# Value products with one 128-column stationary part, division in the merge, and logits in other PSUM banks

## The chip, the core and the metric

The kernel runs on one core of one Trainium2 chip. The metric is the device time in microseconds (us) from start to end of one execution; lower is better. The engines are TensorE (PE, matrix products), VectorE (DVE), ScalarE (ACT), GpSimd (POOL) and SyncE (SP, which issues transfers). ACT issues transfers too. All products here are made of float32 parts: a number x is split into a rounded high part and a low part x - high, and a product is the sum of high x high, high x low and low x high.

## The reference

One layer of a streaming encoder on 1088 frames (1024 of a prompt, 64 of a sample behind 128 cached ones), width 1024:

```python
h = x + 0.5 * swiglu(x, ffn1)
u = rms(h, mix_norm); z = u @ w_in              # q, k, v, indexer, conv input, gates
# attention: every query keeps its best keys by an indexer score (at most 256)
logits = einsum('bqcgd,bqncd->bqcgn', qg, kg) * HEAD_DIM ** -0.5
logits = where(valid, logits, -inf)
p = softmax(logits)
attn = einsum('bqcgn,bqncd->bqcgd', p, vg)      # 8 heads of 64, 2 key/value heads
conv_out = silu(layernorm(depthwise_conv(...))) @ conv_w_out
g_a, g_c = split(sigmoid(gate + b_gate), 2)
h = h + (g_a * (attn @ attn_w_out) + g_c * conv_out) @ w_out
h = h + 0.5 * swiglu(h, ffn2)
```

The change lies in the softmax, in the product with the values, and in how its result reaches `attn @ attn_w_out`.

## The kernel before

Frames are columns in most of the kernel, in three chunks (CHUNKS: 364, 362 and 362 wide, c = 0, 1, 2); the width of 1024 is 8 tiles of 128 partitions. The program goes: first feed-forward block, input projection, indexer scores and the search for the best keys on DVE, attention, second feed-forward block.

Attention runs over nine tiles of queries (eight of 128 in the prompt, number 8 of 64 in the sample; order TORD = 8, 5, 6, 7, 4, 3, 2, 1, 0, tile i with 128(i+1) keys) and, in each, over four pairs of heads. `soft` makes the logits of a pair: L999 and L1000 are the products of the queries with the high and low part of the keys, in a bank of the pool `lg`; L1002 adds the mask (0 or a large negative number) and takes the maximum over the keys on DVE; L1008 joins two halves of the maximum, L1010 scales it, L1012 is the exponential on ACT with its sum, L1014 the reciprocal of the sum on DVE, and L1016 multiplies the exponentials by it, for the first head of the pair on POOL and for the second on DVE. `turn` transposes the probabilities, two blocks of 128 keys at a time (L1026), and splits them into `ph` (ACT, L170) and `pl` (DVE, L171). `values` sums the product with the values in one bank, `pv`, by `mm3` (L154 to L156: high x ph, high x pl, low x ph, each with 64 stationary columns); L1052 copies the sum to `oh` on ACT, and L1053 sends it, from ACT's queue, to `d_at` in memory, head by head.

`attention` interleaves the pairs (logits two pairs ahead, value products two slots behind the transposes) and calls `fill` at each slot, which takes a few steps of a background program: the rest of the gates (L952 tanh on ACT, L953 to `d_g`), the convolution branch (L1132 to L1134, to `d_mp`), then the merge of chunk 2, its output projection, and the merge of chunk 1. A merge waits until the tiles of its chunk are done. It loads the attention result from `d_at` (L1150, `ar`) and splits it into `ah` and `al`, on DVE for even and POOL for odd k (L170, L171). For each of eight tiles m it loads the gate `ga` (L1157) and the convolution part `mpt` (L1159) on SP's queue, multiplies by the weights (`ps` from `ah` and `al`), joins both on DVE (L1162, L1163) and splits into `xh` and `xl` on ACT and DVE. `wout` multiplies these by w_out (24 products for each of 8 tiles m) and adds to h (L1175).

Behind the attention, h comes back from `d_h` in three large loads on ACT's queue (L1252); `wout` of chunk 1, the merge of chunk 0, its `wout` and the second feed-forward follow. Weights stream through `wload` all along: load `raw` on SP (L135), high part `whi` on ACT (L136), low part `wlo` on POOL (L137).

PSUM has eight banks. In the attention, `lg` has three, `psf` (background products) two, `psa` (transposes) two and `pv` one; pools take banks in the order in which they are opened. Each engine runs its own instructions in the order that the compiler's scheduler gives them, and each transfer waits for a completion counter where it takes one over from an earlier transfer; eight such counters are shared by SP's and ACT's queues.

Of the kernel before, what the change touches and what calls it, by code (L numbers as in the profile page):

```python
# [10 lines left out]
F32 = mybir.dt.float32  # L11
F32R = mybir.dt.float32r
# [8 lines left out]
P = 128  # L21
# [14 lines left out]
SC = 'PV'  # L36
# [74 lines left out]
class Kern:  # L111
# [342 lines left out]
    def run(self):  # L454
        tc, nc, a = self.tc, self.nc, self.a
        PS = bass.MemoryType.PSUM
        with ExitStack() as top:
# [10 lines left out]
            d_at = dram.tile([512, T], F32, name="d_at")  # L468
# [466 lines left out]
            vt = ak.tile([P, 2, 10, P], F32R, name="vt")  # L935
# [3 lines left out]
            self.split(vt[:, 0, 0:9, :], vt[:, 1, 0:9, :], raw[:, 0:9, :])  # L939
            self.split(vt[:SMP, 0, 9, :], vt[:SMP, 1, 9, :], raw[:SMP, 9, :])  # L940
# [23 lines left out]
            lgp = self.pool(at_es, "lg", NLG, space=PS)  # L964
            psf = self.pool(at_es, "psf", 7 - NLG - NPT, space=PS)
            psa = self.pool(at_es, "psa", NPT, space=PS)
            pvp = self.pool(at_es, "pv", 1, space=PS)
# [11 lines left out]
            def soft(u):  # L979

                rows, L = u.rows, u.L
                if u.h0 == 0 and u.i not in qts:
                    qts[u.i] = load_q(ak, d_q, u.t0, rows, (ak, ap_)[AORD.index(u.i) % 2], 1)
                qt = qts[u.i]
                nb = 2 if L > 512 else 1
                pw = L // nb
                mb = ap_.tile([P, 8, 2], F32, name="mb", tag="mb", bufs=AHEAD + 1)[:, 0:2, :]
                mx = ap_.tile([P, 2], F32, name="mx", tag="mx", bufs=AHEAD + 1)
                sm = ap_.tile([P, 2], F32, name="sm", tag="sm", bufs=AHEAD + 1)
                u.pr = []  # L990
                kh, kl = K[u.g]
                for hh in range(2):
                    p = ap_.tile([P, 1024], F32, name="pr", tag="pr", bufs=2 * AHEAD + 2)[:rows, :L]
                    u.pr.append(p)
                    q = qt[:, u.h0 + hh, :rows]
                    for b in range(nb):
                        o = lgp.tile([P, 512], F32, name="lg", tag="lg")[:rows, :pw]
                        ks = u.k0 + b * pw
                        nc.tensor.matmul(o, q, kh[:, ks:ks + pw], start=True, stop=False)  # L999
                        nc.tensor.matmul(o, q, kl[:, ks:ks + pw], start=False, stop=True)  # L1000
                        bo = BOFF[u.i] + b * pw
                        nc.vector.tensor_tensor_reduce(p[:, b * pw:(b + 1) * pw], o, bias[:rows, bo:bo + pw],  # L1002
                                                       1.0, -3e38, op0=ALU.add, op1=ALU.max,
                                                       accum_out=mb[:rows, hh, b:b + 1])
                        if (hh, b) == (1, nb - 1):
                            mm = mb[:rows, :, 0]
                            if nb == 2:
                                nc.vector.tensor_tensor(mx[:rows, :], mm, mb[:rows, :, 1], op=ALU.max)  # L1008
                                mm = mx[:rows, :]
                            nc.vector.tensor_scalar(mx[:rows, :], mm, -0.125, None, op0=ALU.mult)  # L1010
                            for e in range(2):
                                nc.scalar.activation(u.pr[e], u.pr[e], AF.Exp, bias=mx[:rows, e:e + 1],  # L1012
                                                     scale=0.125, accum_out=sm[:rows, e:e + 1])
                            nc.vector.reciprocal(sm[:rows, :], sm[:rows, :])  # L1014
                            for e in range(2):
                                {'P': nc.gpsimd, 'V': nc.vector}[SC[e]].tensor_scalar(u.pr[e], u.pr[e], sm[:rows, e:e + 1], None, op0=ALU.mult)  # L1016
                        yield
# [19 lines left out]

            def values(u, slot, ph, pl):
                first, last = slot[0] is u.blocks[0], slot[-1] is u.blocks[-1]
                n = 2 * u.rows  # L1040
                if first:
                    u.pv = pvp.tile([P, 512], F32, name="pv", tag="pv")[:64, 0:n]
                for s_, (vb, kk, kn) in enumerate(slot):
                    vh = vt[:kn, 0, vb, 64 * u.g:64 * u.g + 64]
                    vl = vt[:kn, 1, vb, 64 * u.g:64 * u.g + 64]
                    c = slice(n * s_, n * s_ + n)
                    self.mm3(u.pv, vh, vl, ph[:kn, c], pl[:kn, c], first and s_ == 0, last and s_ == len(slot) - 1)
                if last:
                    if u.h0 == 6:
                        done.add(u.i)  # L1050
                    oh = ap_.tile([64, 256], F32, name="oh", tag="oh", bufs=2)[:, :n]
                    nc.scalar.activation(oh, u.pv, AF.Copy)  # L1052
                    nc.scalar.dma_start(  # L1053
                        d_at[64 * u.h0:64 * u.h0 + 128, u.t0:u.t0 + u.rows].rearrange("(h d) c -> d h c", d=64),
                        oh.rearrange("d (h c) -> d h c", h=2))
# [87 lines left out]
            def merge(c, mp_):  # L1143
# [3 lines left out]
                al = mp_.tile([P, 4, WMAX], F32R, name="al", tag="al")[:, :, :w]  # L1147
                for k in range(4):
                    ar = mp_.tile([P, WMAX], F32, name="ar", tag="ar", bufs=2)[:, :w]
                    nc.sync.dma_start(ar, d_at[k * P:(k + 1) * P, c0:c0 + w])  # L1150
                    self.split(ah[:, k, :], al[:, k, :], ar, nc.gpsimd if k % 2 else nc.vector)
# [284 lines left out]
```

## Time and profile before

| | us |
|---|---|
| median of 3 runs | 2391.95 (2390.51 to 2393.91) |
| the profiled execution | 2394.14 |
| its span, first to last instruction | 2392.3 |
| search ends, first logits start (in the span) | 1151.6, 1157.5 |
| last value product starts | 1535.9 |
| wout of chunk 1 starts, merge of chunk 0 starts | 1540.0, 1574.9 |

The mean granted TensorE clock is 0.987 of full speed, and the chip moved 271.9 MB. The profile is of one execution; where it speaks of busy time, idle time of an engine counts only if another one waits for it.

### The profile page before, as it was taken

The page shows a single profiled execution, that of the slowest core. Times are in us where ns is not written, and L with a number is a line of the kernel's source. Part 1 is how long each engine was busy: PE and PEld are TensorE (multiplying, and loading weights), DVE is VectorE, ACT ScalarE, POOL GpSimd, SP SyncE. Part 2 cuts the span into 40 slices and gives each one's busy share as a digit, 9 for nine tenths or more (in the row PEclk, how much of TensorE's full clock was granted, in tenths as well). Part 3 has the DMA queues.
Part 4 walks back from the last instruction along what each step waited for, and adds up shares of the span by engine and source line. Part 5 has one row for each costly group of instructions (what it writes and reads, how often), then busy time and mean ns, then how long its engine had stood idle before and what let it go on. Part 6 is the DMA issues. An engine that isn't in the chain of part 4 may idle for free.

```text
span 2392.3 us, 43870 instructions
## 1 busy us (share of the span) xinstructions
PE 2300.3 (96%) x16762; PEld 2272.8 (95%) x16762; DVE 1658.8 (69%) x3606; ACT 1146.8 (48%) x2189; POOL 1407.1 (59%) x861
## 2 busy tenths in 40 slices
PE   5999999999999999999899899899999999999997
PEld 5999999999999999999898889899999999999997
DVE  7666678677567387579535897468766678776676
ACT  5433445444335546875644565345433445334343
POOL 4555556555556686889853455457455565445554
PEclk9999999999999999999999999999999999999999
DMA  4232332332223443333322446753232332332223
GB/s 166 89 104 91 98 98 90 125 107 98 89 90 121 143 138 121 91 120 120 106 78 96 125 135 204 254 167 113 80 100 92 107 103 72 108 108 97 89 98 117
DMA packets 130116, 271.90 MB, mean 114 GB/s; under 512 B 18032, under 2 KB 77296, under 8 KB 129904
## 3 DMA queue, kind: packets, MB, share of 16 engines
q1 hardware_dynamic: 114688, 253.48, 32.6%
q10 hardware_dynamic: 15216, 15.60, 2.0%
q8 instruction: 132, 2.16, 0.4%
q14 instruction: 80, 0.66, 0.1%
HBM read 230.34 MB, written 38.75 MB: 112 GB/s over the span
## 4 chain that ended last, share of the span: by engine, by line
PE 76%; DVE 9%; DMA 6%; POOL 4%; issue 2%; ACT 2%; SPq 0%; ACTq 0%; DVEq 0%; POOLq 0%
PE ps L154 24%; PE ps L156 24%; PE ps L155 24%; POOL ac L695 3%; DMA ga<-d_g 1%; PE pt L1026 1%; PE lgi L806 1%; PE lgi L807 1%; DMA d_h<-hr 1%; DVE ga L1163 1%; DMA raw<-wf 1%; DMA raw<-d_k 1%; PE ps L184 1%; DMA d_mp<-gc 1%; DVE t L229 1%
## 5 line engine op out<-in xcount | busy, mean ns | idle before, releaser
L137 POOL TENSOR_TENSOR wlo<-raw,whi 128x1024 fp32r<-128x1024 f32 (+1 forms) x187 | 435.9, 2335 | 352.3 <-ACT whi L136 343.5
L154 PE MATMUL ps<-x,wp 128*128 128x272 f32 x1760 | 508.4, 290 | 10.9 <-DVE spare L302 9.3
L155 PE MATMUL ps<-x,wp 128*128 128x272 f32 x1760 | 506.8, 289 | 0.0
L156 PE MATMUL ps<-x,wp 128*128 128x272 f32 x1760 | 506.1, 291 | 0.8 <-DVE wp L171 0.4
L154 PE MATMUL ps<-x,whi 128*128 128x272 f32 (+2 forms) x1544 | 483.1, 313 | 9.3 <-ACT x L170 4.3
L156 PE MATMUL ps<-x,wlo 128*128 128x272 f32 (+2 forms) x1544 | 481.2, 312 | 0.0
L155 PE MATMUL ps<-x,whi 128*128 128x272 f32 (+2 forms) x1334 | 412.7, 309 | 0.0
L154 PE MATMUL ps<-gh,whi 128*128 128x272 f32 x1408 | 399.8, 289 | 6.8 <-DVE spare L302 5.0
L155 PE MATMUL ps<-gl,whi 128*128 128x272 f32 x1408 | 404.7, 289 | 0.0
L156 PE MATMUL ps<-gh,wlo 128*128 128x272 f32 x1408 | 403.5, 288 | 0.0
L171 POOL TENSOR_TENSOR wlo<-raw,whi 128x1024 fp32r<-128x1024 f32 x88 | 220.4, 2505 | 261.6 <-ACT whi L170 253.2
L154 PEld LDWEIGHTS ps<-x,wp 128*128 128x128 f32 x1760 | 332.9, 189 | 11.7 <-ACT wp L170 11.6
L155 PEld LDWEIGHTS ps<-x,wp 128*128 128x128 f32 x1760 | 333.3, 189 | 0.0
L156 PEld LDWEIGHTS ps<-x,wp 128*128 128x128 f32 x1760 | 330.7, 189 | 2.5 <-DVE wp L171 2.1
L171 POOL TENSOR_TENSOR wp<-s,wp 128x512 fp32r<-128x512 f32 x176 | 256.6, 1458 | 97.2 <-ACT wp L170 97.2
L154 PEld LDWEIGHTS ps<-x,whi 128*128 128x128 f32 x1544 | 293.2, 190 | 11.3 <-ACT x L170 4.7
L136 ACT ACTIVATE whi<-raw 128x1024 fp32r<-128x1024 f32 (+1 forms) x187 | 190.6, 1020 | 218.1 <-PE ps L155 116.8
L156 PEld LDWEIGHTS ps<-x,wlo 128*128 128x128 f32 x1544 | 293.3, 190 | 0.9
L442 DVE SCALAR_TENSOR_TENSOR h<-ps,h 128x272 f32<-128x272 f32 x384 | 164.3, 438 | 184.9 <-PE ps L156 184.4
L695 POOL TENSOR_TENSOR ac<-ac,pd 128x559 f32<-128x559 f32 x180 | 260.9, 1449 | 35.2 <-ACT pd L694 11.8
L154 PEld LDWEIGHTS ps<-gh,whi 128*128 128x128 f32 x1408 | 262.9, 189 | 8.3 <-DVE spare L302 5.7
L156 PEld LDWEIGHTS ps<-gh,wlo 128*128 128x128 f32 x1408 | 265.7, 189 | 0.0
(238 smaller groups left out, 4782.0 us busy)
## 6 DMA issues: line engine op xcount, KB each, us to landing
raw<-wf SPq DMA_DIRECT2D x334, 512.0 KB, 3.3
raw<-wf SPq DMA_DIRECT2D x32, 384.0 KB, 3.1
d_g<-sg ACTq DMA_DIRECT2D x32, 181.0 KB, 1.9
d_h<-h SPq DMA_DIRECT2D x2, 2176.0 KB, 10.4
y<-t SPq DMA_DIRECT2D x32, 136.0 KB, 1.8
raw<-d_q SPq DMA_DIRECT2D x32, 128.0 KB, 2.7
raw<-d_qi SPq DMA_DIRECT2D x24, 128.0 KB, 3.0
d_g<-sg ACTq DMA_DIRECT2D x16, 182.0 KB, 1.9
```

Source lines behind the costliest of these rows:

```text
L136: nc.scalar.activation(hi[:, :n], raw[:, :n], AF.Copy)
L137: self.weng.tensor_tensor(lo[:, :n], raw[:, :n], hi[:, :n], op=ALU.subtract)
L154: t.matmul(out, wh, xh, start=first, stop=False)
L155: t.matmul(out, wh, xl, start=False, stop=False)
L156: t.matmul(out, wl, xh, start=False, stop=last)
L171: (eng or nc.vector).tensor_tensor(lo, x, hi, op=ALU.subtract)
L184: self.nc.tensor.matmul(ps[:, b * P:(b + 1) * P], x[:, t0:t0 + P], self.ones, start=i == 0, stop=i == len(tiles) - 1)
L229: self.nc.vector.scalar_tensor_tensor(x, h[:, k, t0:t0 + w], self.par[:, q:q + 1], r, op0=ALU.mult, op1=ALU.mult)
L442: nc.vector.scalar_tensor_tensor(x, p, 0.5, x, op0=ALU.mult, op1=ALU.add)
L695: nc.gpsimd.tensor_tensor(ac, ac, pd, op=ALU.add)
L806: nc.tensor.matmul(o, qt[:, hd, :], kih[:, ks:ks + pw], start=True, stop=False)
L807: nc.tensor.matmul(o, qt[:, hd, :], kil[:, ks:ks + pw], start=False, stop=True)
```

## The change

One product takes the place of two: the stationary side is now the high and the low part of the values side by side, 64 columns each, so that a product with `ph` gives high x ph in partitions 0 to 63 and low x ph in 64 to 127, and one with `pl` likewise (low x pl comes in too). The two halves go to `d_at` apart, twice the bytes, and are added in the merge.

The probabilities are no longer divided. The reciprocals of a tile's eight heads are collected in `rs`, transposed once a tile on PE, copied on ACT to `rt8` and sent to `d_rs` as rows; the merge loads them over 64 partitions each (`rw`) and multiplies. The merge now has two loads of 64 partitions for each `ar`, an addition and a multiplication for each k, on DVE for even and POOL for odd k. The maximum is found as the minimum of the logits times -0.125, which needs no joining and scaling. `oh` has four buffers for two. The pool `lg` is opened behind `psf` and `psa`, so the three pools swap banks.

```diff
-            d_at = dram.tile([512, T], F32, name="d_at")
+            d_at = dram.tile([8, P, T], F32, name="d_at")
+            d_rs = dram.tile([8, T], F32, name="d_rs")
...
-            vt = ak.tile([P, 2, 10, P], F32R, name="vt")
+            vt = ak.tile([P, 10, 2, 2, 64], F32R, name="vt")
...
-            lgp = self.pool(at_es, "lg", NLG, space=PS)
             psf = self.pool(at_es, "psf", 7 - NLG - NPT, space=PS)
             psa = self.pool(at_es, "psa", NPT, space=PS)
+            lgp = self.pool(at_es, "lg", NLG, space=PS)
...
-                        nc.vector.tensor_tensor_reduce(p[:, b * pw:(b + 1) * pw], o, bias[:rows, bo:bo + pw],
-                                                       1.0, -3e38, op0=ALU.add, op1=ALU.max,
-                                                       accum_out=mb[:rows, hh, b:b + 1])
-                        if (hh, b) == (1, nb - 1):
...
-                            nc.vector.reciprocal(sm[:rows, :], sm[:rows, :])
-                            for e in range(2):
-                                {'P': nc.gpsimd, 'V': nc.vector}[SC[e]].tensor_scalar(u.pr[e], u.pr[e], sm[:rows, e:e + 1], None, op0=ALU.mult)
+                        nc.vector.tensor_tensor_reduce(p[:, b * pw:(b + 1) * pw], o, bias[:rows, bo:bo + pw], -0.125,
+                                                       mn[:rows, hh, 0:1] if b else 3e38,
+                                                       op0=ALU.add, op1=ALU.min, accum_out=mn[:rows, hh, b:b + 1])
+                        if b == nb - 1:
+                            nc.scalar.activation(p, p, AF.Exp, bias=mn[:rows, hh, b:b + 1], scale=-1.0,
+                                                 accum_out=sm[:rows, hh:hh + 1])
+                            if hh:
+                                nc.vector.reciprocal(rs[:, u.h0:u.h0 + 2], sm[:rows, :])
...
-                    self.mm3(u.pv, vh, vl, ph[:kn, c], pl[:kn, c], first and s_ == 0, last and s_ == len(slot) - 1)
+                    vv = vt[:kn, vb, u.g, :, :].rearrange("p a d -> p (a d)")
+                    nc.tensor.matmul(u.pv, vv, ph[:kn, c], start=first and s_ == 0, stop=False)
+                    nc.tensor.matmul(u.pv, vv, pl[:kn, c], start=False, stop=last and s_ == len(slot) - 1)
                 if last:
                     if u.h0 == 6:
                         done.add(u.i)
+                        pt = psa.tile([P, 512], F32, name="pt", tag="pt")[:8, :u.rows]
+                        nc.tensor.transpose(pt, rss[u.i][:u.rows], ident[:u.rows, :u.rows])
+                        rt = ap_.tile([8, P], F32, name="rt8", tag="rt8", bufs=2)[:, :u.rows]
+                        nc.scalar.activation(rt, pt, AF.Copy)
+                        nc.scalar.dma_start(d_rs[:, u.t0:u.t0 + u.rows], rt)
-                    oh = ap_.tile([64, 256], F32, name="oh", tag="oh", bufs=2)[:, :n]
+                    oh = ap_.tile([P, 256], F32, name="oh", tag="oh", bufs=4)[:, :n]
...
+                rs = mp_.tile([P, 4, WMAX], F32, name="rw", tag="rw")[:, :, :w]
+                for e in range(2):
+                    nc.sync.dma_start(rs[64 * e:64 * e + 64],
+                                      d_rs.rearrange("(k e) c -> e k c", e=2)[e:e + 1, :, c0:c0 + w].to_broadcast([64, 4, w]))
                 for k in range(4):
-                    ar = mp_.tile([P, WMAX], F32, name="ar", tag="ar", bufs=2)[:, :w]
-                    nc.sync.dma_start(ar, d_at[k * P:(k + 1) * P, c0:c0 + w])
-                    self.split(ah[:, k, :], al[:, k, :], ar, nc.gpsimd if k % 2 else nc.vector)
+                    ar = mp_.tile([P, 2, WMAX], F32, name="ar", tag="ar", bufs=2)[:, :, :w]
+                    for e in range(2):
+                        nc.sync.dma_start(ar[64 * e:64 * e + 64],
+                                          d_at[2 * k + e, :, c0:c0 + w].rearrange("(a d) c -> d a c", a=2))
+                    eng = nc.gpsimd if k % 2 else nc.vector
+                    eng.tensor_tensor(ar[:, 0, :], ar[:, 0, :], ar[:, 1, :], op=ALU.add)
+                    eng.tensor_tensor(ar[:, 0, :], ar[:, 0, :], rs[:, k, :], op=ALU.mult)
+                    self.split(ah[:, k, :], al[:, k, :], ar[:, 0, :], eng)
```

The code that the diff does not touch keeps its text, but the scheduler gives some of it another place. At the end of the attention ACT's order before is this (`oh` is the copy of the last value products, `d_at<-oh` its transfer, `h<-d_h` the three loads of h, `xh` the split of the merge of chunk 1):

```order
1253 L1052 ACTIVATE oh<-pv 64x256
1254 L170 ACTIVATE ah<-ar 128x364
1255 L1053 DMA d_at<-oh 64x2x128
1256 L170 ACTIVATE xh<-ga 128x362
1257 L1052 ACTIVATE oh<-pv 64x256
1258 L1252 DMA h<-d_h 128x8x362
1259 L1053 DMA d_at<-oh 64x2x128
1260 L1252 DMA h<-d_h 128x8x362
1261 L170 ACTIVATE xh<-ga 128x362
1262 L1252 DMA h<-d_h 128x8x364
1263 L218 ACTIVATE acc<-h 128x272
```

And with the change, at the same place (lines have moved: L1055, L1056 and L1264 are what L1052, L1053 and L1252 were):

```order
1291 L169 ACTIVATE xh<-ga 128x362
1292 L135 ACTIVATE whi<-raw 128x1024
1293 L1055 ACTIVATE oh<-pv 128x256
1294 L1264 DMA h<-d_h 128x8x362 x2
1295 L1056 DMA d_at<-oh 128x2x128
1296 L1264 DMA h<-d_h 128x8x364
1297 L169 ACTIVATE xh<-ga 128x362
1298 L217 ACTIVATE acc<-h 128x272
1299 L169 ACTIVATE xh<-ga 128x362
```

Two loads of h now stand ahead of the last transfer to `d_at`, and two splits of the merge of chunk 1 behind all three. On PE, around the last value product, the order before goes straight on to wout of chunk 1 (operands `xh`, `xl`):

```order
9925 L154 MATMUL pv<-ph,vt 64x256
9926 L155 MATMUL pv<-pl,vt 64x256
9927 L156 MATMUL pv<-ph,vt 64x256
9928 L154 MATMUL ps<-xh,whi 128x362
9929 L155 MATMUL ps<-xl,whi 128x362
9930 L156 MATMUL ps<-xh,wlo 128x362
```

With the change, products of the merge of chunk 1 (operands `ah`, `al`) come first:

```order
9760 L1044 MATMUL pv<-ph,vt 128x256
9761 L1045 MATMUL pv<-pl,vt 128x256
9762 L153 MATMUL ps<-ah,whi 128x362
9763 L154 MATMUL ps<-al,whi 128x362
9764 L155 MATMUL ps<-ah,wlo 128x362
```

What moved is the last two tiles of that merge, 24 products in all, from ahead of the last value product to behind it; wout of chunk 1 follows them. Their loads on SP, in the order with the change (the loads of 362 columns are of chunk 1, m = 6 and 7; those of 364 of chunk 0, where `ar` stands for k = 1, 2 and 3):

```order
287 L1158 DMA ar<-d_at 64x2x364 x2
288 L134 DMA raw<-wf 128x1024
289 L1171 DMA mpt<-d_mp 128x362
290 L1169 DMA ga<-d_g 128x362
291 L1171 DMA mpt<-d_mp 128x362
292 L1169 DMA ga<-d_g 128x362
293 L1158 DMA ar<-d_at 64x2x364 x2
294 L134 DMA raw<-wf 128x1024
295 L1158 DMA ar<-d_at 64x2x364 x2
```

Before, the last loads of 362 columns stand ahead of the second half of the `ar` loads, and nothing of a load of h is waited for in front of them:

```order
281 L1150 DMA ar<-d_at 128x364
282 L1159 DMA mpt<-d_mp 128x362 x2
283 L1157 DMA ga<-d_g 128x362
284 L1150 DMA ar<-d_at 128x364
285 L135 DMA raw<-wf 128x1024
286 L1157 DMA ga<-d_g 128x362
287 L1159 DMA mpt<-d_mp 128x364
```

In the changed program as built, the mpt loads in rows 289 and 291 wait on the completion counters that the first and the second load of h raise, the raw load in row 294 on that of the third.

More of the change, by code (lines that the diff above doesn't have):

```diff
@@ L938, in run @@
             nc.sync.dma_start(raw[:SMP, 9, :], d_v[:SMP, 9, :])
-            self.split(vt[:, 0, 0:9, :], vt[:, 1, 0:9, :], raw[:, 0:9, :])
-            self.split(vt[:SMP, 0, 9, :], vt[:SMP, 1, 9, :], raw[:SMP, 9, :])
+            for g in range(2):
+                for r, b in ((P, slice(0, 9)), (SMP, slice(9, 10))):
+                    self.split(vt[:r, b, g, 0, :], vt[:r, b, g, 1, :], raw[:r, b, 64 * g:64 * g + 64])
             AORD = TORD
@@ L986, in soft @@
                 pw = L // nb
-                mb = ap_.tile([P, 8, 2], F32, name="mb", tag="mb", bufs=AHEAD + 1)[:, 0:2, :]
-                mx = ap_.tile([P, 2], F32, name="mx", tag="mx", bufs=AHEAD + 1)
+                mn = ap_.tile([P, 2, 2], F32, name="mn", tag="mn", bufs=AHEAD + 1)
                 sm = ap_.tile([P, 2], F32, name="sm", tag="sm", bufs=AHEAD + 1)
+                if u.h0 == 0:
+                    rss[u.i] = ap_.tile([P, 8], F32, name="rs", tag="rs", bufs=2)
+                rs = rss[u.i][:rows]
                 u.pr = []
@@ L1036, in turn @@
                 return ph, pl
+            rss = {}
             def values(u, slot, ph, pl):
@@ L1041, in values @@
                 if first:
-                    u.pv = pvp.tile([P, 512], F32, name="pv", tag="pv")[:64, 0:n]
+                    u.pv = pvp.tile([P, 512], F32, name="pv", tag="pv")[:, 0:n]
                 for s_, (vb, kk, kn) in enumerate(slot):
-                    vh = vt[:kn, 0, vb, 64 * u.g:64 * u.g + 64]
-                    vl = vt[:kn, 1, vb, 64 * u.g:64 * u.g + 64]
                     c = slice(n * s_, n * s_ + n)
-                    self.mm3(u.pv, vh, vl, ph[:kn, c], pl[:kn, c], first and s_ == 0, last and s_ == len(slot) - 1)
+                    vv = vt[:kn, vb, u.g, :, :].rearrange("p a d -> p (a d)")
+                    nc.tensor.matmul(u.pv, vv, ph[:kn, c], start=first and s_ == 0, stop=False)
+                    nc.tensor.matmul(u.pv, vv, pl[:kn, c], start=False, stop=last and s_ == len(slot) - 1)
                 if last:
@@ L1050, in values @@
                         done.add(u.i)
-                    oh = ap_.tile([64, 256], F32, name="oh", tag="oh", bufs=2)[:, :n]
+                        pt = psa.tile([P, 512], F32, name="pt", tag="pt")[:8, :u.rows]
[4 more added lines that the diff above has]
+                    oh = ap_.tile([P, 256], F32, name="oh", tag="oh", bufs=4)[:, :n]
                     nc.scalar.activation(oh, u.pv, AF.Copy)
                     nc.scalar.dma_start(
-                        d_at[64 * u.h0:64 * u.h0 + 128, u.t0:u.t0 + u.rows].rearrange("(h d) c -> d h c", d=64),
-                        oh.rearrange("d (h c) -> d h c", h=2))
+                        d_at[u.h0:u.h0 + 2, :, u.t0:u.t0 + u.rows].rearrange("h p c -> p h c"),
+                        oh.rearrange("p (h c) -> p h c", h=2))
             def attention(units, fill):
```

9 lines of the change are left out of this document (removed).

## The prediction, made before the changed kernel was run

> **What bounds the kernel now.** First the head of the page and its chain of waits; then busy time by stage, for the stretch that the change touches: the attention with its background work (1150 to 1540 us of the span) and the start of what follows.
>
> ```profile
> span 2392.3 us, 43870 instructions
> PE 2300.3 (96%) x16762; PEld 2272.8 (95%) x16762; DVE 1658.8 (69%) x3606; ACT 1146.8 (48%) x2189; POOL 1407.1 (59%) x861
> PE 76%; DVE 9%; DMA 6%; POOL 4%; issue 2%; ACT 2%; SPq 0%; ACTq 0%; DVEq 0%; POOLq 0%
> ```
>
> TensorE (PE) is busy for 96% of the span and holds 76% of the chain, so over the whole run an edit counts by the PE time that it frees. In the stretch at issue that isn't so everywhere (columns: stretch and its length; busy us of PE, its weight loads, DVE, ACT and POOL, that is VectorE, ScalarE and GpSimd; granted clock, DMA share, GB/s):
>
> ```profile
> 1160.00:1290.00 130.00, 130.00 (x835) 126.45 (x835) 51.05 (x140) 69.23 (x134) 72.93 (x43) 0.99 0.27 84
> 1290.00:1420.00 130.00, 115.81 (x824) 107.04 (x822) 117.60 (x302) 81.90 (x170) 63.13 (x31) 1.00 0.45 135
> 1420.00:1490.00 70.00, 66.36 (x425) 64.78 (x425) 55.93 (x132) 37.50 (x90) 38.52 (x24) 0.96 0.56 174
> 1490.00:1540.00 50.00, 41.96 (x248) 40.43 (x246) 25.74 (x39) 18.21 (x32) 27.39 (x14) 0.95 0.68 218
> ```
>
> Call the rows A, B, C and D. In A, PE is never idle. In B DVE is busy for 117.60 of 130 us and PE stands still for 14.2. In C and D PE stands still for 11.7 us, and most of what it waits for is this (between 1150 and 1620 us: total, times, longest):
>
> ```profile
> PE ps L154 <- DVE ga L1162: 7.8, 5, 3.8
> PE pv L154 <- ACT oh L1052: 6.7, 4, 3.5
> ```
>
> **The value products.** The order of the changed kernel has two products of 256 columns where there were three (304 for 456), each with 128 stationary columns for 64. How many stood in each stretch (PE, weight loads, ACT), and how far apart products start:
>
> ```profile
> 1160.00:1290.00 130.00, 15.27 (x113) 13.16 (x114) 2.54 (x8) 0.99 0.27 84
> 1290.00:1420.00 130.00, 41.02 (x250) 29.93 (x248) 5.14 (x14) 1.00 0.45 135
> 1420.00:1490.00 70.00, 12.05 (x72) 9.25 (x71) 2.92 (x8) 0.96 0.56 174
> 1490.00:1540.00 50.00, 3.93 (x24) 2.91 (x24) 2.19 (x6) 0.95 0.68 218
> ```
>
> ```profile
> 1244.76 0.28 PE L154 MATMUL pv<-ph,vt 128*64 128x256 f32 x1
> 1245.35 0.28 PE L156 MATMUL pv<-ph,vt 128*64 128x256 f32 x1
> 1699.87 0.29 PE L154 MATMUL ps<-x,whi 128*128 128x272 f32 x1
> 1701.38 0.29 PE L154 MATMUL ps<-x,whi 128*128 128x272 f32 x1
> ```
>
> Between the first two rows lie five steps (0.118 us each), between the others, with 128 stationary and 272 moving columns, twelve (0.126 us): 0.46 ns a moving column in both, so the wider load lies under the product before it. I take it at 0 to 3 ns each (under 1 us in all). A third of the products is freed: 113/3 x 0.118 = **4.4 us in A**, 9.8 in B, 3.8 in C and D.
>
> One rule speaks against this edit. The Trainium skill, "TensorE: Matmul & The Clock Gate", section "LDWEIGHTS (loading the stationary operand)", has the load grow with its columns, at P/1.2 ns: 53 ns for 64, 107 for 128 (an estimate by that page). Were it not hidden, 304 x 53 ns = 16 us would eat what 152 fewer products save (rival 4). The trace agrees on the growth but shows the longer load hidden, with its 0.126 us a step.
>
> **The normalisation.** The change takes away the 36 + 36 multiplications at L1016 and the maxima and scalings at L1008 and L1010. Their cost in B, L1016 (DVE, then POOL) and L1010 (DVE); then the spread of L1010 (ns: least, median, most) and that of operations like those that come:
>
> ```profile
> 1290.00:1420.00 130.00, 8.15 (x13) 32.99 (x14) 1.00 0.45 135
> 1290.00:1420.00 130.00, 5.05 (x14) 1.00 0.45 135
> L1010 DVE TENSOR_SCALAR mx<-mb x20: 151/306/2342, 1160.6 to 1515.1; 128x2 f32<-128x2 f32 x16, 64x2 f32<-64x2 f32 x4
> L171 DVE TENSOR_TENSOR al<-ar,ah x6: 525/538/1683, 1341.0 to 1549.3; 128x362 fp32r<-128x362 f32 x4, 128x364 fp32r<-128x364 f32 x2
> L171 POOL TENSOR_TENSOR al<-ar,ah x6: 970/1099/1258, 1354.7 to 1559.7; 128x362 fp32r<-128x362 f32 x4, 128x364 fp32r<-128x364 f32 x2
> ```
>
> In B DVE loses 8.15 + 5.05 = 13.2 us and the few of L1008. The merge's additions and multiplications come in its place: 12 on DVE and 12 on POOL, of the shape of the last two rows, some 4 of DVE's in B: 2.2 us, 3 with stretching as in the 1683 ns case. DVE is 10.2 us shorter, PE 9.8. Between 9.8 (PE alone gains) and 24 (its 14.2 idle us go as well) I take **14 us in B**, near the DVE figure plus some of the 32.99 us of POOL that go from the path from reciprocal to transpose. That an operation on two elements took 2342 ns, where 151 is the least, shows what DVE suffers from something beside it.
>
> The Trainium skill, "SBUF — State Buffer", section "Who interferes with whom", names POOL's exclusive lock on a port pair as the cause of such stretching. By it POOL's 33 us would give DVE time back beyond its own instructions. The 2342 ns agree; how much it is, no run here shows (rival 5).
>
> In C and D: 3.8 for the products plus some of the 11.7 idle us. But there SP's loads for the merge double in number (ar: two of 64 partitions for one of 128, and rw) and wait for landings ahead of the ga and mpt loads that PE waits for (first row of the waits). Between 0 and 13 I take **6.5**.
>
> **The start.** The 6.9 us at L999 end with the last tanh of the gates:
>
> ```profile
> 1157.50 0.42 PE L999 MATMUL lg<-kh,qt 128*64 128x192 f32 x1 [6.88 <-ACT sg L952]
> 1158.52 0.56 PE L154 MATMUL ps<-x,whi 128*128 128x364 f32 x1
> ```
>
> With the logits in other banks the six between these rows no longer wait for it. The gates' product of the second row does, since its pool takes the banks that the logits had; only 1.02 us move: **1 us** (0 to 1.5).
>
> **Small costs.** Nine transposes of reciprocals, with a wait each, and the wider loads: **1.7 us** (0.6 to 3). ACT's nine copies and DMA issues lie beside PE; where ACT is late they cost what the L1052 waits cost now, within those bounds.
>
> **The tail.** This is the term that decides. Rows of PE, ACT's queue, ACT and DVE behind the last value product, SP's wait for h loads, and a ga load's time to landing:
>
> ```profile
> 1535.93 0.28 PE L156 MATMUL pv<-ph,vt 128*64 128x256 f32 x1
> 1539.98 0.64 PE L154 MATMUL ps<-xh,whi 128*128 128x362 f32 x1 [3.77 <-DVE ga L1162]
> 1574.69 0.33 PE L156 MATMUL ps<-xh,wlo 128*128 128x362 f32 x1
> 1574.85 0.33 PE L154 MATMUL ps<-ah,whi 128*128 128x364 f32 x1
> ...
> 1537.96 0.57 ACTq L1252 DMA_DIRECT2D h<-d_h  x1
> 1540.44 5.10 ACTq L1252 DMA_DIRECT2D h<-d_h  x1
> 1548.08 0.43 ACT L218 ACTIVATE acc<-h 128x272 f32<-128x272 f32 x1 [7.14 <-DMA h<-d_h]
> 1554.98 0.98 DVE L1175 SCALAR_TENSOR_TENSOR h<-ps,h 128x362 f32<-128x362 f32 x2 [4.05 <-DMA h<-d_h]
> ```
>
> ```profile
> SPq L1159 <- DMA h<-d_h: 4.5, 1, 4.5
> ```
>
> ```profile
> ga<-d_g SPq DMA_DIRECT2D x2, 181.0 KB, 3.2
> ```
>
> Before, the wout products of chunk 1 start 4.05 us after the last value product and last 34.9, up to the first merge product of chunk 0. All loads that they need were issued ahead of the h loads, which land 10.1 us (the first) and 17.0 (the second) after the first was issued. In the order of the changed kernel two merge tiles of chunk 1 (m = 6 and 7: 24 products, 3.9 us by the step of 0.16 from 1574.69 to 1574.85) stand behind the last value product, and their loads behind h: as the kernel is built, SP's mpt load of m = 6 waits for the completion counter that h load 1 raises, that of m = 7 for h load 2's, with ga of m = 7 behind it. The row of SP's waits shows it in such a wait already. The first h load is issued 0.8 us behind the last value product, with one copy ahead of it (2.0 before), so h load 2 lands 14 to 18 us behind it (14 if less traffic beside it makes it quicker), the two loads 3.2 us later, two DVE steps and a split some 1.3 more: wout starts 18.5 to 22.5 us after the last value product, and its 34.9 us end at 53.4 to 57.4 where they ended at 38.9. That is **16.5 us lost** (11 if the loads have the queues to themselves, 20 if SP is late as well). The 3.9 us of merge products stood ahead of the last value product before and now lie inside this wait, so the stretch ahead is shorter by **3.9 us**. Nothing else fills the wait, since PE keeps its order.
>
> **Sum.** -4.4 - 14 - 6.5 - 1 - 3.9 + 1.7 + 16.5 = -11.6 us. Against the profiled execution (2394.14 us, of which 2392.3 is span) that is 2382.5; it lies 2.19 us above the median of 2391.95, so the time forecast is **2380 us**.
>
> **Rivals.**
> 1. The tail is hidden: the h loads land early, or the counters don't couple. For it: SP, held up, sends little beside them. Against it: 10.1 and 17.0 us above. All but the tail remains, -28.1: 2364 us. Chance 0.15.
> 2. Only PE's own saving counts, and DVE's and POOL's relief comes to nothing, since new loads on SP take over as what PE waits for. For it: five waits for ga, 7.8 us. Against it: DVE's 90% in B. -4.4 - 9.8 - 3.8 - 1 - 3.9 + 1.7 + 16.5 = -4.7: 2387 us. Chance 0.18.
> 3. Slower: the tail grows at one place. In the changed order SP's load of ar for k = 3 stands behind a weight load that waits for h load 3 (issued 1540.44 and landed 21.0 us later, below), and POOL does that part's add, multiply and split ahead of twelve weight splits. wout's fifth tile, due 16 us after wout starts (36.6 us behind the last value product), needs the first of these. h load 3 lands 0.8 + 2.5 + 21.0 = 24.3 us behind that product if it lands as before, ar 4.7 later and with its issue at about 30; POOL's own part of 3 to 4 us and one split of 2.4 make 36.4: just in time. Each us later costs one. From a landing at 46.5 on (11.6 to lose, and 4.8 more) it decides; at 50 it gives 2400 us. For it: d_at's traffic doubles (2.2 to 4.4 MB each way). Against: in the rows of before only h itself lands so late. Chance 0.13.
>
> ```profile
> h<-d_h ACTq DMA_DIRECT2D x1, 1456.0 KB, 21.0
> ar<-d_at SPq DMA_DIRECT2D x4, 182.0 KB, 4.7
> 1557.33 2.40 POOL L137 TENSOR_TENSOR wlo<-raw,whi 128x1024 fp32r<-128x1024 f32 x1 [2.33 <-ACT whi L136]
> ```
>
> 4. The weight loads aren't hidden. A load of 64 columns takes 134 ns, one of 128 takes 190, so 304 x 56 ns = 17 us come back: 2397 us. Against it: the steps of 0.126 us above. Chance 0.04.
>
> ```profile
> L154 PEld LDWEIGHTS pv<-ph,vt x152: 129/134/223, 1179.2 to 1535.6; 128*64 128x64 f32 x148, 64*64 64x64 f32 x4
> L154 PEld LDWEIGHTS ps<-x,whi 128*128 128x128 f32 x1544 | 293.2, 190 | 11.3 <-ACT x L170 4.7
> ```
>
> 5. POOL's work is what stretches DVE, so that all of PE's idle time in B goes with it: 24 us there for 14. For it: 2342 ns against 151. Against it: POOL gets 12 of the merge's additions and multiplications and keeps its 2.4 us weight splits. 2370 us. Chance 0.10.
>
> That the change doesn't do what it says is out: its order has 304 products on 128 columns.
>
> **From these to the numbers.** Forecast 0.40 (2373 to 2386 by itself). Of that nearly all is faster by over 0.2%, which is 4.8 us and about what a measurement of this kernel tells from no change; of rival 2 under half. Faster 0.38 + 0.15 + 0.07 + 0.10 = 0.70; same 0.02 + 0.11 + 0.02 (the edge of 3) = 0.15; slower 0.11 + 0.04 = 0.15. The range leaves out the quick half of rival 1 and the far part of 3 and 4: 2363 to 2395.
>
> **What would show it.** In the changed profile: value products x304 starting every 0.12 us (else rival 4); DVE in the second stretch well under 117 us and few PE waits there; the first wout product 18 to 23 us behind the last value product, with PE idle most of it and the wait ending with DVE's ga, and SP waiting for h<-d_h. If PE is idle there for under 5 us, rival 1 holds and the time is near 2364. If wout itself stops at its fifth tile for POOL's wlo, it's rival 3. If the stretch up to the last value product is shortened by under 22 us, the terms for B, C and D are wrong.

## The result, and the profile after

| | before | changed |
|---|---|---|
| median, 4 runs each (us) | 2391.23 (2384.43 to 2393.91) | 2412.54 (2408.60 to 2416.82) |
| ratio, 95% interval | | 1.0094 (1.0066 to 1.0121) |
| profiled execution, its span (us) | 2394.14, 2392.3 | 2408.60, 2406.8 |

The changed kernel is 0.94% slower, some 21 to 22 us (21.3 by the medians, 22.5 by the ratio); 2380 was forecast, with a range up to 2395. The profiled execution of the changed kernel is the fastest of its four, 3.9 us below their median.

The head of its page, the busy rows of the same stretches as before, and the longest waits of PE between 1150 and 1640 us:

```profile
PE 2297.5 (95%) x16619; PEld 2269.4 (94%) x16619; DVE 1625.7 (68%) x3532; ACT 1149.7 (48%) x2200; POOL 1355.7 (56%) x837
```

```profile
1160.00:1290.00 130.00, 130.00 (x822) 126.33 (x820) 40.43 (x113) 70.75 (x142) 52.13 (x32) 0.99 0.30 96
1290.00:1420.00 130.00, 114.01 (x746) 105.05 (x745) 113.77 (x277) 82.77 (x176) 34.06 (x22) 0.95 0.51 147
1420.00:1490.00 70.00, 59.53 (x368) 57.29 (x367) 43.39 (x104) 34.59 (x87) 26.39 (x14) 0.95 0.68 195
1490.00:1540.00 50.00, 42.71 (x233) 41.78 (x231) 14.90 (x24) 14.40 (x22) 25.64 (x12) 0.87 0.82 241
```

```profile
PE ps L153 <- DVE ga L1174: 19.9, 6, 8.6
PE ps L153 <- ACT sg L953: 5.5, 1, 5.5
PE pt L1022 <- DVE pl L170: 4.5, 6, 2.1
PE ps L153 <- DVE hr L1187: 3.2, 1, 3.2
```

The reader is to see three things. PE has 143 products less, and DVE and POOL are busy for less time, as intended (PE's busy time falls by 2.8 us only, since a product that runs slower counts as longer). In the second stretch DVE is still busy for 113.77 of 130 us, and PE's granted clock is 0.95 where it was 1.00. And the waits for ga went from 7.8 to 19.9 us.

To see where the time went, both traces were cut at equal work: the products other than value products and reciprocals' transposes are the same in both, so their moving columns were counted from 1115 us on, where the two run alike. The table (worked out from all PE rows of the two traces) gives for each stretch of the kernel before the time that the same work took in each. "own" is the value products and reciprocals at their usual step, "idle" PE's idle time, "slow" what products took above their usual step, at a lower clock or for another reason.

```
stretch of before   before: took  own  idle slow   changed: took  own  idle slow   difference
1160 to 1290        129.9  12.2   0.0   6.2        127.2   9.0   0.0   6.5          -2.7
1290 to 1420        130.3  28.7  14.2  12.1        128.9  19.1  16.0  18.3          -1.4
1420 to 1490         69.8   8.2   3.6   6.5         77.4   6.5  10.5   9.0          +7.6
1490 to 1520         29.7   1.4   0.6   0.9         31.9   0.7   2.8   1.7          +2.2
1520 to 1550         30.0   1.4   7.4   5.3         41.5   0.2  16.1   9.3         +11.5
```

At 1160 us the two were level (0.1 us), at 1550 the changed kernel is 17 us behind. In the second stretch 9.6 us of products are gone and 8.0 come back as idle and slow time. The third loses 7.6 us, the end 11.5. Over the five stretches 16.4 us of products are saved, PE is idle for 19.6 us more, and slow time is 13.8 us more.

Such a cut is of one execution, and neighbouring stretches trade time when the order changes: e4 below, which as a whole takes as long as the kernel before, is by the same cut 6.0 us shorter in the second stretch and 6.8 us longer in the third. So a stretch shows where time went in that execution; what an edit costs is read from the whole times.

The end, first on PE, then on ACT's queue, ACT and DVE, then SP's waits for h between 1525 and 1580 us:

```profile
1531.14 0.28 PE L1044 MATMUL pv<-ph,vt 128*128 128x256 f32 x1
1531.26 0.28 PE L1045 MATMUL pv<-pl,vt 128*128 128x256 f32 x1
1535.60 0.67 PE L153 MATMUL ps<-ah,whi 128*128 128x362 f32 x1 [4.05 <-DVE ga L1174]
1542.99 0.67 PE L153 MATMUL ps<-ah,whi 128*128 128x362 f32 x1 [3.40 <-DVE ga L1174]
1555.61 0.64 PE L153 MATMUL ps<-xh,whi 128*128 128x362 f32 x1 [8.63 <-DVE ga L1174]
1590.64 0.33 PE L153 MATMUL ps<-ah,whi 128*128 128x364 f32 x1
...
1531.64 0.59 ACTq L1264 DMA_DIRECT2D h<-d_h  x1
1533.78 6.28 ACTq L1056 DMA_DIRECT2D d_at<-oh  x1
1544.09 0.43 ACT L217 ACTIVATE acc<-h 128x272 f32<-128x272 f32 x1 [2.17 <-DMA h<-d_h]
1533.80 1.30 DVE L1162 TENSOR_TENSOR ar<-ar,rw 128x364 f32<-128x364 f32 x1 [6.15 <-DMA rw<-d_rs]
1541.96 0.54 DVE L170 TENSOR_TENSOR xl<-ga,xh 128x362 fp32r<-128x362 f32 x1 [5.84 <-ACT xh L169]
1554.93 0.53 DVE L1174 SCALAR_TENSOR_TENSOR ga<-ga,ps 128x362 f32<-128x362 f32 x1 [3.08 <-DMA ga<-d_g]
```

```profile
SPq L1171 <- DMA h<-d_h: 10.1, 2, 7.4
```

wout of chunk 1 starts 24.4 us behind the last value product (4.05 before; 18.5 to 22.5 forecast) and its end, the first merge product of chunk 0, lies 59.4 us behind it (38.9 before; 53.4 to 57.4 forecast). SP's mpt loads wait for the h loads, as the order showed, and the last and longest of PE's three waits (8.63 us) ends with them, when ga of m = 7 has landed. The first two have other sources that the forecast hadn't: DVE's multiplication for the next merge waits 6.15 us for rw ahead of the eviction for which PE waits until 1535.60; and the d_at transfer holds ACT's queue for 6.28 us, with the split xh behind it, for which DVE waits 5.84 us ahead of the eviction for which PE waits until 1542.99.

In the third stretch, rows of DVE and PE, and DVE's longest wait between 1420 and 1490 us:

```profile
1484.57 0.54 DVE L1161 TENSOR_TENSOR ar<-ar 128x362 f32<-128x362 f32 x1 [5.39 <-DMA ar<-d_at]
1485.60 0.53 DVE L1187 SCALAR_TENSOR_TENSOR hr<-ps,hr 128x362 f32<-128x362 f32 x1
1486.18 0.67 PE L153 MATMUL ps<-xh,whi 128*128 128x362 f32 x1 [3.24 <-DVE hr L1187]
```

```profile
DVE ar L1161 <- DMA ar<-d_at: 8.2, 2, 5.4
```

DVE's new addition waits for ar ahead of the eviction L1187, and PE for that eviction, 3.24 us. DVE has no wait for ar or rw between 1420 and 1490 us in the kernel before.

### The profile page after: what moved, and what is told of

Same layout as the page of the kernel before. It is cut to its first block, busy times and chain, and to the rows that moved or that the text cites. A ratio compares the mean times of both kernels' runs of the same rounds, so it can differ in the third digit from the quotient of the medians.

```text
span 2406.8 us, 43499 instructions
## 1 busy us (share of the span) xinstructions
PE 2297.5 (95%) x16619; PEld 2269.4 (94%) x16619; DVE 1625.7 (68%) x3532; ACT 1149.7 (48%) x2200; POOL 1355.7 (56%) x837
## 4 chain that ended last, share of the span: by engine, by line
PE 78%; DVE 9%; DMA 6%; POOL 3%; issue 2%; ACT 2%; SPq 0%; ACTq 0%; DVEq 0%; POOLq 0%
PE ps L153 25%; PE ps L155 24%; PE ps L154 24%; POOL ac L695 3%; DMA ga<-d_g 1%; PE pt L1022 1%; DVE pl L170 1%; PE lgi L806 1%; PE lgi L807 1%; DMA h<-d_h 1%; DVE ga L1175 1%; PE ps L183 1%; DVE pr L1005 1%; DMA raw<-d_k 1%; DVE t L228 1%
```

## The experiments

All were timed in five rounds against the kernel before; "x us" is the ratio times 2392. Comparisons of two experiments are good to some 4 us, the width of their intervals. Where an edit makes the order of h fixed, it is this one (m = 7 is the last tile of the merge of chunk 1):

```diff
+        self.hi = nc.scalar.activation(hi, x, AF.Copy)            # in split
...
+                    if (c, m) == (1, 7):
+                        self.mark = self.hi                       # in merge
...
+                self.behind(nc.scalar.dma_start(h[...], d_h[...]), self.mark)
```

### The tail, the products, the division and the banks apart

e1_h_last is the changed kernel with that edit.

> The changed kernel; only the three loads of h are issued behind the last ACT split of the merge of chunk 1 (m = 7). Theory A: the wait behind the last value product comes from the h loads in front of the last d_at transfer and from the ga and mpt loads of m = 6 and 7 that wait for them. Then wout of chunk 1 starts 6 to 10 us after the last value product (24.5 in the changed kernel), the first merge product of chunk 0 40 to 46 us after it (59.4), and the time falls by 12 to 18 us, to 2395 to 2400 us. Rival: merge loads are late because of their own number and traffic, wherever h stands: wout still starts 18 us or more after the last value product, and the time stays within 5 us of the changed kernel's 2412.

Measured: 1.0050 (1.0032 to 1.0068), +12 us, so 10 us of the loss are gone, less than the 12 to 18 that were expected. By equal work the end from 1520 to 1550 us took 31.9 us, 41.5 in the changed kernel. PE and DVE there:

```profile
1532.66 0.28 PE L1050 MATMUL pv<-pl,vt 128*128 128x256 f32 x1
1539.35 0.67 PE L153 MATMUL ps<-ah,whi 128*128 128x362 f32 x1 [6.41 <-DVE ga L1179]
1549.40 0.64 PE L153 MATMUL ps<-xh,whi 128*128 128x362 f32 x1 [4.38 <-ACT xh L174]
1538.32 0.54 DVE L1167 TENSOR_TENSOR ar<-ar,rw 128x364 f32<-128x364 f32 x1 [6.24 <-DMA rw<-d_rs]
1538.77 0.52 DVE L1179 SCALAR_TENSOR_TENSOR ga<-ga,ps 128x362 f32<-128x362 f32 x1
```

wout starts 16.7 us after the last value product (24.4 with h first), not 6 to 10: h was a part of that wait. The wait of 6.41 us that is left ends with the eviction L1179, which stands behind the merge's multiplication on DVE, and that waited 6.24 us for rw. The other 12 us of the loss remain.

e2_h_last_zero gives e1 a third product again:

```diff
-                    nc.tensor.matmul(u.pv, vv, pl[:kn, c], start=False, stop=last and ...)
+                    nc.tensor.matmul(u.pv, vv, pl[:kn, c], start=False, stop=False)
+                    nc.tensor.matmul(u.pv, vz[:kn], ph[:kn, c], start=False, stop=last and ...)
```

> As e1_h_last, with a third product in each value step again: 128 zero columns as the stationary part, so that it adds nothing to the result. PE has as many value products as before the change. Theory B: in the stretch from 1290 to 1490 us the 152 products saved are worth next to nothing, since DVE and loads set its pace and a thinner PE stream is granted a lower clock (0.83 in stretches of 10 us). Then this one is within 5 us of e1_h_last, and the granted clock is 0.98 or more from 1290 to 1420 us. Rival: the saved products count in full and something else eats the gain: this one is 15 to 18 us slower than e1_h_last.

Measured: 1.0075 (1.0056 to 1.0094), 6 us above e1: between the two forecasts, and nearer to theory B: the 152 products cost a third of their 17.8 us (152 steps of some 0.117 us). By the cut at equal work the second stretch took 129.6 us with them and 132.8 without; the clock there was 0.97 and 0.93.

e3_division_only leaves out of the change the products, the halves and the banks: `mm3`, `oh` and `d_at` as before, and one multiplication by `rw` in the merge.

> The kernel before, with only the division moved into the merge (reciprocals as rows, minimum for maximum, multiplication in the merge); value products, d_at and PSUM banks as before. Theory of the prediction: without DVE's 44 us and POOL's 67 us the stretch from 1290 to 1490 us gets shorter by 5 to 10 us: 2381 to 2387 us. Rival: that work lay beside the path: within 3 us of before. Second rival: waits for rows of reciprocals and for the DVE multiplication in front of evictions cost more than it brings: 2395 us or more.

Measured: 1.0008 (0.9999 to 1.0016). The 44 us of DVE and 67 us of POOL are gone, and nothing is gained: the rival. By equal work the second stretch took 128.3 us (130.3 before), with 4.7 us less idle and 2.8 more slow time, in an execution that was 6.8 us below the median.

e4_banks_only opens the logits' pool last, in the kernel before.

> The kernel before, with only the pool of the logits opened last, so that the banks change. Theory: at most 1 us, as the lag between the traces at 1160 us of the span is 0.1 us: 2389 to 2393 us. Rival: the banks steer the later order too, 5 us or more either way.

Measured: 1.0003 (0.9994 to 1.0012). The banks are worth nothing, though the order that comes of them moves 6 us from the second stretch to the third, as said above.

### The halves

e5_products_only_h_last has the change's products and halves with the softmax and division of before (L1016 back, no `rw`), h fixed.

> The kernel before with only the value products of the change (128 stationary columns, both halves through d_at, added in the merge), softmax, division and banks as before; h loads behind the merge as in e1_h_last. Theory C: between 1420 and 1530 us the halves through d_at cost some 13 us (e1_h_last and e2_h_last_zero lose 12 to 14 there by the lag of the traces, e3_division_only none): twice the ar loads and a DVE addition that waits for them in front of evictions that PE waits for. Then this one is at 2396 to 2406 us, like e1_h_last. Rival: the rows of reciprocals and their multiplication do it together with the halves: 2380 to 2390 us.

Measured: 1.0096 (1.0079 to 1.0114), +23 us: above both forecasts. So moving the division, worth nothing by itself, is worth 11 us beside the cheaper products (e5 to e1; the banks differ too, and e4 has them at nothing).

e6_sum_at_eviction_h_last adds the halves as they leave PSUM, in the changed kernel:

```diff
-                    nc.scalar.activation(oh, u.pv, AF.Copy)
+                    nc.scalar.activation(oh, u.pv[0:64], AF.Copy)
+                    nc.vector.tensor_tensor(oh, oh, u.pv[64:128], op=ALU.add)
```

> The changed kernel with the halves added where they leave PSUM (ACT copies partitions 0 to 63, DVE adds 64 to 127), so that d_at, its transfers and the ar loads are as before the change; the division stays in the merge; h loads behind the merge. Theory C: the loss between 1420 and 1530 us goes, 10 us or more below e1_h_last: 2384 to 2393 us. Rival: the loss stays (it comes from the rows of reciprocals, or from merge work that falls later in PE's order): 2399 us or more.

Measured: 1.0021 (1.0009 to 1.0033), +5 us, 7 us below e1, between the two forecasts. By equal work the third stretch took 70.9 us where e1 took 78.1, but this execution was 7.2 us below the median of e6. Adding the halves in the merge, with the transfers that it needs, costs 7 us more than adding them here.

e7_products_sum_h_last is the same with the old softmax and division.

> The kernel before with the two products of 128 columns and the halves added where they leave PSUM; softmax, division, d_at and banks as before; h loads behind the merge. By theories A to C the saved products count where PE sets the pace (4.4 us up to 1290 us, 3.8 us behind 1420 us), nothing between: 2381 to 2389 us. Rival, by which any thinning of PE's work is lost to waits: 2391 us or more.

Measured: 1.0063 (1.0040 to 1.0086), +15 us. The gain of 4.4 + 3.8 us that was expected isn't there; something eats saved products even without the halves in memory (DVE has 36 additions more here, and all of the old softmax). Against e5 it is 8 us faster: the place of the addition is worth as much with the old softmax as with the new one. By equal work its third stretch took 84.0 us, 14 more than in the kernel before, though no addition stands in its merge.

e11_merge_on_pool_h_last moves the merge's DVE work of e1 to POOL (`eng = nc.gpsimd`).

> e1_h_last with the merge's additions, multiplications and low parts of all k on POOL, none on DVE; the halves go through d_at as in the changed kernel. Theory C1: the loss behind 1420 us comes from DVE's addition, which waits for ar ahead of evictions for which PE waits; it goes, and the time is 2390 to 2396 us. Rival C2: the loss comes from the transfers themselves (twice as many ar loads in front of ga and mpt on SP): the time is that of e1_h_last, 2400 to 2406 us.

Measured: 1.0017 (1.0008 to 1.0026), 8 us below e1, at the upper end of the range of C1. The halves still go through memory, so it is the merge's work on DVE, which waits for loads in front of evictions, more than the traffic, that costs these 8 us. How they divide between additions, multiplications and low parts isn't shown, since all three moved. By equal work the third stretch took 71.6 us, in an execution 3.8 us below the median; that the 8 us lie there alone isn't shown either, as e4 and e7 lose time there without such an addition.

e8_before_h_last fixes h in the kernel before.

> The kernel before with the h loads behind the last ACT split of the merge of chunk 1. There the loads stand in front of one transfer only, and nothing of the merge of chunk 1 waits for them: within 4 us of before. Rival: h first is dear in the kernel before too, 5 us or more faster.

Measured: 1.0004 (0.9994 to 1.0015). The early h loads cost the kernel before nothing.

### What a product is worth

e9_before_two_products leaves the third product out of the kernel before (with h fixed), and e10_before_four_products adds a fourth with zeros:

```diff
-                    self.mm3(u.pv, vh, vl, ph[:kn, c], pl[:kn, c], ...)
+                    nc.tensor.matmul(u.pv, vh, ph[:kn, c], start=first and s_ == 0, stop=False)
+                    nc.tensor.matmul(u.pv, vh, pl[:kn, c], start=False, stop=last and ...)
```

> e8_before_h_last with the third value product (low x ph) simply left out, so 304 products of 64 stationary columns and nothing else changed; the result lacks that part. It measures what 152 products are worth by themselves. Theory B, bounded by waits between 1290 and 1490 us: 4 to 10 us faster than e8_before_h_last, all of it before 1290 and behind 1490 us. Rival D, thinning alone costs (clock granted below 1.00 in more slices, attention running ahead of the background in PE's order): as slow as e8_before_h_last or slower. Rival E, products count in full: 16 to 18 us faster.

> e8_before_h_last with a fourth value product (64 zero columns as the stationary part, which adds nothing): 608 products. Theory B: 4 to 10 us slower, not the 17.8 us of 152 products. Rival D: within 3 us or faster, with the clock at 1.00 from 1290 to 1490 us.

Measured: e9 1.0012 (1.0002 to 1.0022), e10 1.0047 (1.0034 to 1.0060). With nothing added in their place, 152 products fewer made the kernel no faster; 152 more cost 10 us of their 17.8. Here are 10 us of the kernel before and of e9:

```profile
1320.00:1330.00 10.00, 8.49 (x59) 7.46 (x58) 10.00 (x24) 5.29 (x14) 2.81 (x4) 1.00 0.04 8
```

```profile
1320.00:1330.00 10.00, 7.38 (x36) 6.29 (x37) 9.94 (x22) 4.82 (x12) 4.17 (x5) 0.83 0.08 20
```

DVE is full in both, and in e9 the clock is 0.83 for 1.00. The traces give the clock in windows of some 3.41 us, and in each of them it is either 1.00 or 0.50. Three of these windows of e9, and the first of them in the kernel before:

```profile
1320.10:1323.50 3.40, 1.73 (x6) 0.89 (x6) 3.40 (x10) 1.10 (x2) 0.15 (x1) 1.00 0.00 0
1323.50:1326.90 3.40, 2.81 (x12) 2.84 (x13) 3.40 (x6) 2.53 (x9) 2.08 (x3) 0.50 0.00 0
1326.90:1330.30 3.40, 3.13 (x22) 2.85 (x21) 3.34 (x9) 1.19 (x3) 1.84 (x2) 1.00 0.32 85
```

```profile
1320.10:1323.50 3.40, 2.80 (x21) 2.18 (x19) 3.40 (x8) 1.46 (x3) 0.00 (x0) 1.00 0.09 19
```

PE was busy for half of the first window in e9, with DVE full, and the next window ran at half the clock; with 2.80 of 3.40 us busy in the kernel before, it didn't. From 1290 to 1490 us e9's clock was 0.93 and 0.95, e8's 0.98 and 0.96.

### What holds the second stretch

e12_sum_lag3 (e6 with LAG 3), e13_sum_ahead3 (e6 with AHEAD 3) and e14_before_lag3 (e8 with LAG 3) change one number each.

> e6_sum_at_eviction_h_last with the value products three slots behind their transposes (LAG 3 for 2, one more pair of ph and pl buffers). Theory F: between 1290 and 1420 us PE waits for the chain from logits over minimum, exponential, transposes and splits to the products, one step at a time, so that work taken off PE, DVE or POOL there only lengthens the waits; one slot more of distance takes waits away: 4 us or more below e6_sum_at_eviction_h_last (2398 us). Rival G: PE waits for the layer norm of the background (its own chain between DVE, ACT and PE), which the distance doesn't change: within 3 us.

> e6_sum_at_eviction_h_last with the logits three pairs ahead of the transposes (AHEAD 3 for 2, two more buffers of probabilities). Theory F: 4 us or more below e6_sum_at_eviction_h_last. Rival G: within 3 us.

> e8_before_h_last with the value products three slots behind their transposes. Theory F: 4 us or more faster than e8_before_h_last (2394 us), since its waits in that stretch (14.2 us idle) are of the same kind. Rival G: within 3 us.

Measured: 1.0020 (1.0009 to 1.0032), 1.0073 (1.0057 to 1.0089) and 1.0004 (0.9995 to 1.0014). Against e6, e6 and e8 that is nothing, 12 us worse, and nothing: theory F falls.

e15_before_thin_norm cuts the background's norm (`tanh`, bias and the two DVE operations behind it left out) in e8, e16 in e9, e17 in e1.

> e8_before_h_last with the layer norm of the background cut: its bias, tanh and swish (8 DVE operations of 128x392 and 4 on ACT for each of three chunks) are left out. Theory G: this chain sets the pace between 1290 and 1420 us; without some 17 us of DVE and three hops between DVE and ACT a chunk, 8 us or more go: 2386 us or less. Rival: it doesn't, within 4 us of e8_before_h_last.

> e15_before_thin_norm with the third value product left out as in e9_before_two_products. Theory G: once the norm no longer sets the pace, saved products count: 8 us or more faster than e15_before_thin_norm (e9 against e8 was 3 us slower). Rival D: thinning is lost to waits and clock wherever it falls: within 4 us of e15.

> e1_h_last with the layer norm cut in the same way. Theory G: 10 us or more below e1_h_last (2403 us), and no more than 5 us above e15_before_thin_norm. Rival: the halves in the merge still cost their 8 us and more: 8 us or more above e15_before_thin_norm.

Measured: e15 1.0002 (0.9992 to 1.0012), e16 0.9939 (0.9924 to 0.9954), e17 0.9997 (0.9988 to 1.0006). The first expectation failed: less norm alone brings nothing. But with less norm the saved products bring 15 us (e15 to e16), and the changed kernel 13 (e1 to e17). The second stretch of e16:

```profile
1290.00:1420.00 130.00, 116.79 (x793) 106.33 (x792) 116.27 (x287) 78.18 (x163) 64.86 (x35) 1.00 0.46 138
```

793 matmuls get done there, 715 in e9, and the clock stays at 1.00. A doubt remains on where the 15 us come from. In e15 the order moved some 40 value products out of the second stretch, so that by equal work it won 13 us there against the kernel before and lost 13 from 1490 to 1520 us. In the second stretch e16 was no faster than e15 (118.3 us for 116.9); 12 of the 15 us lie between 1490 and 1520. So a part of them may be e15's order.

e18_sum_lag3_norm_on_pool gives half of the norm's operations behind the tanh to POOL, in e12.

> e12_sum_lag3 with half of the layer norm's bias, swish product and sum (t = 0 and 2) on POOL, as three operations each, in place of two on DVE: nothing is left out. If easing DVE's part of the norm is what saved products need (e16 against e15), 5 us or more below e12_sum_lag3 (2396 us), so faster than before. Rival: POOL's slower operations make the norm's chain longer, and the time stays or rises.

Measured: 1.0045 (1.0033 to 1.0058), 6 us worse than e12. No version with the whole norm was faster than the kernel before.

## Why the prediction was wrong

- **The start** (1 us): 0.1 us by equal work, and e4 shows nothing. The gates' product, which keeps its wait, was the one that counted.
- **The first stretch** (4.4 us): 2.7. Right in kind; the value products of that part of the work fell by 3.2 us only, since some moved in from later.
- **The second stretch** (14 us): 1.4, and this step failed. It took PE's 9.8 us as the least that could be won, though the row that it quoted had DVE busy for 117.60 of 130 us and PE idle for 14.2; a product that is saved where PE waits for others lengthens the wait. And it took DVE's 10.2 us as the rest, as if one engine's freed time shortened a stretch in which others are late as well. e3 shows that DVE's and POOL's part alone gives nothing, e9 that PE's part alone gives nothing, e5 against e1 that the former gives 11 us when the latter is there. Neither was a term of a sum.
- **The clock** was no term at all, though it is a part of that step's miss: 18.3 us of slow time in the second stretch for 12.1. The changed kernel around the first of its drops there:

```profile
1329.10:1332.50 3.40, 1.66 (x13) 1.35 (x12) 2.42 (x6) 0.67 (x2) 2.12 (x1) 1.00 0.88 239
1332.50:1335.90 3.40, 3.40 (x16) 3.40 (x15) 2.24 (x8) 1.84 (x4) 0.00 (x0) 0.50 0.52 138
1335.90:1339.30 3.40, 3.40 (x27) 3.38 (x27) 1.30 (x3) 1.47 (x3) 0.00 (x0) 1.00 0.78 285
```

  PE, busy for half of the first window, gets half the clock in the second and does 16 products there, 27 in the third. Half of PE's busy time in such windows, as an estimate of what the clock cost, is 5.5 us in the second stretch, 0.2 in the kernel before, and so most of the 6.2 us by which slow time grew. From 1160 to 1550 us it is 20.5 us for 8.7. The Trainium skill, "TensorE: Matmul & The Clock Gate", section "Part 1: The HAM clock gate", has the clock at half after at least one idle window of about 3.4 us. The length of the windows agrees; but the window ahead of this drop wasn't idle, as PE was busy for 1.66 of its 3.40 us. That the lower clock decides the loss is not shown, since it follows PE's waits and no run here changed it by itself.
- **The third and fourth stretch** (6.5 us gained): 9.8 lost. The bounds were 0 and 13, and the step failed by its lower end: it named the doubled loads but let them only reduce a gain. What it left out is that the merge's new work on DVE waits for these loads in front of evictions that PE waits for; e6 and e11 take that away in two ways, and the whole time falls by 7 and 8 us. That all of it lies in these stretches is not shown.
- **The sign that the prediction named** for these terms came: it called them wrong if the stretch up to the last value product is shortened by under 22 us, and that product starts at 1531.26 us for 1535.93, 4.7 us earlier.
- **The tail** (16.5 lost, 3.9 gained): right in mechanism. By equal work it cost 11.5 us, and 16.5 less 3.9, that is 12.6, were forecast; measured from the last value product, the end of wout came 20.5 us later, where 16.5 were forecast. e1 gives 10 us of it back. Its parts were near: h load 2 landed some 16.5 us behind the last value product (14 to 18 forecast; SP issues the mpt load that waits for it at 1547.73 us), but ga of m = 7 then took 6.8 us, for which 3.2 had been taken. It was the term the prediction called decisive, and it was the one that held.
- **The wider weights**: no cost of their own is seen; in the changed kernel value products follow each other at 0.12 us (1531.14 to 1531.26).

The rival for slower (one place in the tail, from ar for k = 3) isn't what happened: wout takes 35.0 us from its start to the first merge product of chunk 0, 34.9 before. Taken off one after the other, the 21 to 22 us are 10 for the h loads (e1), 7 to 8 for the halves in the merge and its work on DVE (e6, e11), and 4 to 5 that are left in e6 and e11, each good to some 4 us. That rest, and the gain of over 20 us ahead of the tail that never came, go with saved work that brings nothing by itself (e3, e9) and with a lower clock. What holds the second stretch is settled only in part: it isn't the attention's look-ahead (e12 to e14), it isn't the norm alone (e15). That products, softmax and norm bound it together is the reading that fits e5 to e1 and e9 to e16, and no more than that.

## What to carry to other kernels

Where the bound engine idles and another is nearly full in the same stretch, work taken off either one may be worth nothing by itself, as here, and its lower bound in a forecast is zero or below. Where a merge gets an operation that waits for a transfer, look at what stands behind it on its engine. And read a changed order at the stage's end: here two large loads that moved ahead of one small transfer cost nearly half of the loss.

## What the runs showed of the hardware

- PE's granted clock falls without a long idle. In the 20 profiles of this case (all PE rows and clock windows from 1165 to 1600 us) it fell 101 times from 1.00 to 0.50. In the window ahead PE was always busy for less than 0.67 of the time; wherever it was busy for less than 0.44, the clock fell; between these bounds it fell or stayed. In 65 of the 101 no single wait in that window was longer than 2.5 us.
- Taking 152 products out of the kernel before brought its clock from 0.98 to 0.93 between 1290 and 1420 us (e8 to e9).
- One transfer's issue held ACT's queue for 6.28 us behind two loads of 1.48 MB (changed kernel, 1533.78 us).
